# Attention with 16 heads: the scores of a pair's two heads issued in turns on the two halves of the array's rows

## The chip, the core and the metric

The kernel runs on one core of a Trainium2 chip. A core has TensorE (PE, matmuls and transpositions, results go to PSUM), VectorE (DVE), ScalarE (ACT), GpSimd (POOL) and a queue that starts DMAs (SP). The metric is the time of one execution on the device in microseconds (us): the median of three runs before the change is 2080.74 us (2080.17 to 2080.78).

## What is computed

Two transformer-like blocks run one after the other on 512 tokens of width 1024. The change is in one stage of the second block, an attention with 16 heads of 64 columns. Instead of a softmax it takes, for every query, products of sigmoids over the keys that lie between a key and the query ("stick breaking"):

```python
z = jnp.einsum("bhqd,bhkd->bhqk", qb, k32) * scale
mask = key_pos[None, :] < q_pos[:, None]
log_beta = jax.nn.log_sigmoid(z)
log_1m = jnp.where(mask, jax.nn.log_sigmoid(-z), 0.0)
suffix = lax.cumsum(log_1m, axis=3, reverse=True) - log_1m
wts = jnp.where(mask, jnp.exp(log_beta + suffix), 0.0)
return jnp.einsum("bhqk,bhkd->bhqd", wts, v32)
```

The output of all heads is then multiplied with `w_out` and added to the residual `x`. The mask is strictly causal, so a block of 128 queries needs only the key blocks up to its own.

## The kernel before

Activations lie transposed, features on the 128 partitions and the 512 tokens in the free dimension. All matmuls of weights are made three times over parts of numbers (`hi` and `lo` of type float32r): `mm3` issues lo times hi, hi times lo, hi times hi. A slab of 1024x128 weights is loaded by SP (`raw`), copied to `whi` by ACT (L101) and reduced to `wlo` by DVE (L102). `Feed` holds the order of all slabs and runs two to three ahead.

The attention stage works on pairs of heads: pair k (0 to 7) is one slab of 128 columns of q, of k and of v, and a head of it is one half of the 128 partitions (`p0 = 64 * half`). For each pair there are these steps:

- `proj(k, w)`: 24 matmuls of 128x512 (trace names `psmm`) for q and k; v is the same in two parts of 12 (`psv`). `evac` (L1164 to L1172) takes the result out of PSUM: ACT and DVE make `qh`, `ql`, `kh`, `kl`, and the tile `qk`.
- `scores(half, ...)`: for one head 12 matmuls with 64 rows into three PSUM tiles `z0`, `z1`, `z2` (L1119): three each over 512, 384, 128 and 256 columns, 3840 in all. Behind each of the three groups of columns ACT makes sigmoids `om` and `be` (L1124), POOL masks the diagonal blocks (L1128), DVE scans (`pr`, L1131) and multiplies (`be`, L1134). This chain of one head is called its mixing below.
- `turn(be)`: 10 transpositions of 128x128 (`t`, L1146), taken out as `w0h` to `w2l` by ACT and DVE.
- `values(k, half, ...)`: 12 matmuls of 128 rows with v (`po`, L1157); only the head's 64 rows of the result are taken out (`Oh`, `Ol`, L1161 and L1162).
- `vparts(t)`: four transpositions of v (`pv`, L1182), taken out as `vh` (ACT) and `vl` (DVE).
- `out_part(m, ks)`: 21 or fewer matmuls of the output projection (`pso`), put in where the last pairs have nothing to project.

PSUM: the pool `pmm3` has two buffers with the tag `mm`, used in turns by the `psmm`, `psv`, `po` and `pv` tiles: a new tile waits until the tile two before it has been taken out. `psz` holds `z0` to `z2`, `t0` and `t1`, and `pn` one tile `nr` for `t2`.

The order on PE is the order of the code (`manual_schedule` for PE). The order on the other engines is set at build time by a scheduler with an estimated time line, and then stands; each engine works through its own queue in order.

In the loop before (L1200 to L1226) the two heads are shifted against each other: while PE turns and multiplies one head, the mixing of the other one runs. PE does, for a pair: scores of head 1, turn head 0, project the next k, values of head 0, half of the next v, scores of the next pair's head 0, turn head 1, the other half of v, project the q after next, values of head 1, `vparts`.

Of the kernel before, what the change touches and what calls it, by code (L numbers as in the profile page):

```python
# [9 lines left out]
F32 = mybir.dt.float32  # L10
# [6 lines left out]
P = 128  # L17
T = 512
KD = 8
# [34 lines left out]
def block_kernel(ctx: ExitStack, tc: tile.TileContext, xT, pT, cols, cst, wA, wBr, wO, w13, w2, wPG, wPL,  # L54
                 aIn, aRI, aO, bQKV, bO, f13, f2, outT, dbg=None, upto=99):
    nc = tc.nc
    V, S, G, TE = nc.vector, nc.scalar, nc.gpsimd, nc.tensor
# [10 lines left out]
    pn = ctx.enter_context(tc.tile_pool(name="pn", bufs=1, space=PSUM))  # L68
# [71 lines left out]
    feed = Feed()  # L140
# [18 lines left out]
    feed.add([aO[m] for m in range(KD)])  # L159
    feed.mark((0, 0, 1))  # L160
    ffn_plan(f13[0], f2[0])
    feed.add([bQKV[8], bQKV[9], bQKV[0], bQKV[10]])
    for k in range(KD - 1):
        feed.add([bQKV[9 + 2 * (k + 1)], bQKV[k + 1]] + ([bQKV[8 + 2 * (k + 2)]] if k < KD - 2 else []))
    feed.mark((2, 0, 0, 1))
    feed.add([bO[m] for m in range(KD)])
    feed.mark((0, 0, 1))
# [9 lines left out]
    def gemm(pool, src, xs, tag="mm"):  # L177
        hi, lo = feed.next(src)
        ps = pool.tile([P, T], F32, tag=tag, name="psmm")
        mm3(ps, [(hi[:, k, :], lo[:, k, :], xs[k]) for k in range(len(xs))])  # L180
        return ps
# [106 lines left out]
    with ExitStack() as ca:  # L288
# [297 lines left out]
        for h in range(H):  # L586
            p0 = (h % 2) * 64
            Sm = ML.tile([P, 1280], F32, tag="Sm", bufs=1, name="Sm")
            for j in range(NB):
                w = T - j * P  # L590
# [481 lines left out]
    with ExitStack() as cs:  # L1072
# [27 lines left out]
        def parts(name, src, w, bufs):  # L1100
            hi = SB.tile([P, w], F32R, tag=name + "h", bufs=bufs, name=name + "h")
            lo = SB.tile([P, w], F32R, tag=name + "l", bufs=bufs, name=name + "l")
            S.copy(hi[:, 0:w], src)
            V.tensor_tensor(lo[:, 0:w], src, hi[:, 0:w].bitcast(F32), op=ALU.subtract)
            return hi, lo

        def scores(half, qp, kp):

            p0 = 64 * half
            zs = [psz.tile([P, T], F32, tag=f"z{g}", name=f"z{g}") for g in range(3)]  # L1110
            be = SB.tile([P, 1280], F32, tag="be", bufs=2, name="be")
            om = SB.tile([P, 1280], F32, tag="om", bufs=2, name="om")
            pr = SB.tile([P, 1280], F32, tag="pr", bufs=1, name="pr")
            for g in range(3):
                qbs = [(i, o, w) for g_, i, o, w in QB if g_ == g]
                for i, o, w in qbs:
                    qs = slice(p0, p0 + 64), slice(i * P, (i + 1) * P)
                    for n, (a, b) in enumerate(((0, 1), (1, 0), (0, 0))):
                        TE.matmul(zs[g][:, o:o + w], qp[a][qs], kp[b][p0:p0 + 64, 0:w], start=(n == 0 and o == 0),  # L1119
                                  stop=(n == 2), skip_group_check=True)  # L1120
                c0, cw = ZW[g]
                for t, n in ((om, 1), (be, 0)):
                    for i, o, w in qbs:
                        S.activation(t[:, c0 + o:c0 + o + w], zs[g][:, o:o + w], AF.Sigmoid, scale=rq[:, n, i:i + 1])  # L1124

                    d0 = c0 + qbs[0][1] + qbs[0][2] - P
                    d = t[:, d0:c0 + cw].rearrange("p (n c) -> p n c", c=P)
                    G.affine_select(d, d, pattern=[[0, len(qbs)], [-1, P]], base=0, channel_multiplier=1,  # L1128
                                    compare_op=ALU.is_gt, fill=float(n))
                sl = slice(c0, c0 + cw)  # L1130
                V.tensor_tensor_scan(pr[:, sl][:, ::-1], om[:, sl][:, ::-1], anew[:, sl][:, ::-1], 1.0,  # L1131
                                     op0=ALU.mult, op1=ALU.max)

                V.tensor_tensor(be[:, c0:c0 + cw - 1], be[:, c0:c0 + cw - 1], pr[:, c0 + 1:c0 + cw], op=ALU.mult)  # L1134
            return be

        def turn(be):

            out = []
            for g, (w, js) in enumerate(ZG):  # L1140
                t = pn.tile([P, T], F32, tag="nr", name="t2") if g == 2 else psz.tile([P, T], F32, tag=f"t{g}", name=f"t{g}")
                for j in js:
                    for i in range(j, NB):
                        c = next(ZW[g_][0] + o for g_, i_, o, _ in QB if i_ == i) + j * P
                        o = ZP[j][1] + (i - j) * P
                        TE.transpose(t[:, o:o + P], be[:, c:c + P], ident)  # L1146
                out.append(parts(f"w{g}", t[:, 0:w], w, 1))
            return out

        def values(k, half, wts, vp, pool=pmm, tag="mm"):  # L1150
            po = pool.tile([P, T], F32, tag=tag, name="po")
            n = 0
            for g in range(3):
                for j in ZG[g][1]:
                    o = ZP[j][1]
                    for (a, b) in ((1, 0), (0, 1), (0, 0)):
                        TE.matmul(po[:, j * P:], vp[a][:, j, :], wts[g][b][:, o:o + NW[j]], start=(n == 0), stop=(n == 11),  # L1157
                                  skip_group_check=True)
                        n += 1
            s_ = slice(64 * half, 64 * half + 64)  # L1160
            S.copy(O[k][0][s_], po[s_])  # L1161
            V.tensor_tensor(O[k][1][s_], po[s_], O[k][0][s_].bitcast(F32), op=ALU.subtract)  # L1162
# [4 lines left out]
        def evac(ps, w):  # L1167

            if w == 0:
                return parts("q", ps, T, 2)  # L1170
            t = tp.tile([P, T], F32, tag="xin", bufs=3, name="qk")
            V.tensor_tensor(t, ps, R, op=ALU.mult)  # L1172
            return t if w == 2 else parts("k", t, T, 2)

        def proj(k, w):

            return evac(gemm(pmm, bQKV[8 + 2 * k + w] if w < 2 else bQKV[k], A), w)

        def vparts(t):
            pv = pmm.tile([P, NB, P], F32, tag="mm", name="pv")  # L1180
            for b in range(NB):
                TE.transpose(pv[:, b, :], t[:, b * P:(b + 1) * P], ident)  # L1182
            return [x.rearrange("p (b d) -> p b d", b=NB) for x in parts("v", pv.rearrange("p b d -> p (b d)"), T, 2)]
# [3 lines left out]
        def out_part(m, ks, pool=pmm, tag="mm"):  # L1187

            if m not in part:
                part[m] = feed.next(bO[m]) + (pool.tile([P, T], F32, tag=tag, name="pso"),)  # L1190
            hi, lo, ps = part[m]
            mm3(ps, [(hi[:, c, :], lo[:, c, :], O[c]) for c in ks], first=ks[0] == 0, last=ks[-1] == KD - 1)

        with tc.manual_schedule(engines={mybir.EngineType.PE}):
            q, kk = proj(0, 0), proj(0, 1)
            vt = proj(0, 2)
            wa = scores(0, q, kk)
            qn = proj(1, 0)
            v = vparts(vt)
            for k in range(KD):  # L1200
                more = k < KD - 1
                wb = scores(1, q, kk)
                wt = turn(wa)
                if more:
                    kk, q = proj(k + 1, 1), qn
                    values(k, 0, wt, v)
                    vhi, vlo = feed.next(bQKV[k + 1])
                    pv = pmm.tile([P, T], F32, tag="mm", name="psv")
                    mm3(pv, [(vhi[:, c, :], vlo[:, c, :], A[c]) for c in range(4)], last=False)
                    wa = scores(0, q, kk)  # L1210
                    wt = turn(wb)
                    mm3(pv, [(vhi[:, c, :], vlo[:, c, :], A[c]) for c in range(4, 8)], first=False)
                    vt = evac(pv, 2)
                    if k < KD - 2:
                        qn = proj(k + 2, 0)
                    else:
                        out_part(0, range(0, 6))
                    values(k, 1, wt, v)
                    v = vparts(vt)
                else:  # L1220
                    out_part(1, range(0, 7))
                    values(k, 0, wt, v, psz, "z0")
                    out_part(0, range(6, 7))
                    wt = turn(wb)
                    out_part(2, range(0, 7), psz, "z1")
                    values(k, 1, wt, v, psz, "z0")  # L1226
            out_part(3, range(0, 7), psz, "z2")
            for m in range(4):
                out_part(m, range(7, 8))
        ss = SumSq("ss7")  # L1230
        for m in range(KD):
            ps = part[m][2] if m in part else gemm(psz, bO[m], O, tag=("z0", "t0", "t1", "z1")[m % 4])
            V.tensor_tensor(x_tiles[m], ps, x_tiles[m], op=ALU.add)
            split_scaled(A[m], x_tiles[m], col("nf1", m))
            ss.add(x_tiles[m])
# [168 lines left out]
```

## Time and profile before

| | before |
|---|---|
| median of three runs | 2080.74 us |
| the profiled execution, time | 2082.17 us |
| its span | 2080.2 us |
| PE busy | 2051.9 us (99%) |
| DVE busy | 1104.5 us (53%) |
| ACT busy | 763.9 us (37%) |
| POOL busy | 257.1 us (12%) |
| the chain of work that ended last | PE 91%, DVE 5%, ACT 1%, rest below |

The profile is of one execution. Busy time counts what an engine executes; matmuls are pipelined, so the pace of PE is read from the distance of starts, not from the duration of one. The granted clock says at which share of 2.4 GHz PE ran (0.5 is 1.2 GHz). The attention stage is the stretch from the first score matmul at 1451.17 us to the last partial output product, after which the rest of the output projection begins at 1683.42 us.

### The profile page before, as it was taken

The numbers are of one execution on the slowest core, as the hardware profiler recorded it, in microseconds if no ns is written. First come the engines' busy times: TensorE is split into PE (matmuls) and PEld (weight loads), VectorE is DVE, ScalarE is ACT, GpSimd is POOL, SyncE is SP. The second block draws the span as 40 slices with busy tenths as digits, with TensorE's granted clock in tenths as the row PEclk, the third lists the DMA queues.
The fourth block names the chain that finished last, engine by engine and source line by source line (L and its number), as shares of the span: only waits on it lengthen the run. The fifth ranks groups of instructions, "written<-read, shape, count | busy, mean of one in ns | idle before, by whom it ended". The sixth has DMA issues, their size and how long they took to land.

```text
span 2080.2 us, 24373 instructions
## 1 busy us (share of the span) xinstructions
PE 2051.9 (99%) x9786; PEld 1705.2 (82%) x9786; DVE 1104.5 (53%) x1455; ACT 763.9 (37%) x1099; POOL 257.1 (12%) x266
## 2 busy tenths in 40 slices
PE   8999999999999999999899999999999999999998
PEld 7778899888888888887788888888888888888887
DVE  5667453554444423669964444333877754444322
ACT  4334232333232322546642323223555533322221
POOL 0111000131000000252320000001322220000011
PEclk9999999999999999999999999999999999999999
DMA  4211111343333333322323333333122123333332
GB/s 168 71 55 59 60 41 43 105 127 101 97 96 100 91 97 98 114 79 82 91 91 96 97 101 92 92 101 98 55 61 72 41 77 96 91 102 94 92 102 68
DMA packets 53664, 181.69 MB, mean 87 GB/s; under 512 B 5808, under 2 KB 7984, under 8 KB 53552
## 3 DMA queue, kind: packets, MB, share of 16 engines
q1 hardware_dynamic: 53408, 180.05, 28.9%
q8 instruction: 76, 1.25, 0.3%
q14 instruction: 36, 0.29, 0.0%
q10 hardware_dynamic: 144, 0.10, 0.0%
HBM read 178.03 MB, written 2.10 MB: 87 GB/s over the span
## 4 chain that ended last, share of the span: by engine, by line
PE 91%; DVE 5%; ACT 1%; issue 1%; POOL 1%; DMA 1%; SPq 0%; POOLq 0%; DVEq 0%; ACTq 0%
PE psmm L173 19%; PE psmm L174 19%; PE psmm L175 19%; PE psd L173 6%; PE psd L175 6%; PE psd L174 6%; PE z L1119 2%; PE po L1157 1%; DVE wlo L102 1%; PE pU L731 1%; PE pX L726 1%; PE t L1146 1%; DVE xc L987 1%; PE psv L173 1%; PE psv L174 1%
## 5 line engine op out<-in xcount | busy, mean ns | idle before, releaser
L101 ACT CAST whi<-raw 128x1024 fp32r<-128x1024 f32 (+1 forms) x333 | 344.5, 1036 | 942.3 <-issue 374.5
L102 DVE TENSOR_TENSOR wlo<-raw,whi 128x1024 fp32r<-128x1024 f32 (+1 forms) x333 | 411.0, 1235 | 287.9 <-ACT whi L101 287.8
L173 PE MATMUL psmm<-Bh,wlo 128*128 128x512 f32 x1032 | 402.3, 390 | 0.3 <-DVE Ol L1162 0.3
L174 PE MATMUL psmm<-Bl,whi 128*128 128x512 f32 x1032 | 402.2, 390 | 0.1
L175 PE MATMUL psmm<-Bh,whi 128*128 128x512 f32 x1032 | 402.1, 390 | 0.0
L173 PE MATMUL psmm<-Ah,wlo 128*128 128x512 f32 x832 | 332.9, 401 | 2.8 <-DVE wlo L102 1.9
L175 PE MATMUL psmm<-Ah,whi 128*128 128x512 f32 x832 | 325.2, 391 | 0.0
L174 PE MATMUL psmm<-Al,whi 128*128 128x512 f32 x832 | 324.4, 390 | 0.6 <-DVE Al L189 0.6
L173 PEld LDWEIGHTS psmm<-Bh,wlo 128*128 128x128 f32 x1032 | 193.8, 188 | 40.8 <-DVE Ol L1162 0.5
L175 PEld LDWEIGHTS psmm<-Bh,whi 128*128 128x128 f32 x1032 | 193.8, 188 | 40.3
L174 PEld LDWEIGHTS psmm<-Bl,whi 128*128 128x128 f32 x1032 | 193.8, 188 | 40.2 <-DVE Bl L189 0.5
L216 POOL TENSOR_TENSOR ss<-ss,sq 128x512 f32<-128x512 f32 x55 | 85.6, 1561 | 1141.7 <-issue 803.7
L173 PE MATMUL psd<-Hh,wlo 128*128 128x512 f32 x506 | 196.8, 389 | 0.0
L174 PE MATMUL psd<-Hl,whi 128*128 128x512 f32 x506 | 196.8, 389 | 0.0
L175 PE MATMUL psd<-Hh,whi 128*128 128x512 f32 x506 | 196.8, 389 | 0.0
L173 PEld LDWEIGHTS psmm<-Ah,wlo 128*128 128x128 f32 x832 | 156.3, 188 | 36.0 <-DVE wlo L102 3.2
L175 PEld LDWEIGHTS psmm<-Ah,whi 128*128 128x128 f32 x832 | 156.1, 188 | 33.6
L174 PEld LDWEIGHTS psmm<-Al,whi 128*128 128x128 f32 x832 | 156.6, 188 | 30.3 <-DVE Al L189 1.1
L870 DVE TENSOR_TENSOR u<-psmm,R 128x512 f32<-128x512 f32 x66 | 45.6, 691 | 194.2 <-PE psmm L175 194.2
L866 DVE TENSOR_TENSOR s<-psmm,R 128x512 f32<-128x512 f32 x66 | 45.7, 692 | 137.0 <-PE psmm L175 134.0
L175 PEld LDWEIGHTS psd<-Hh,whi 128*128 128x128 f32 x506 | 95.0, 188 | 19.8
L174 PEld LDWEIGHTS psd<-Hl,whi 128*128 128x128 f32 x506 | 95.0, 188 | 19.8
(468 smaller groups left out, 2475.9 us busy)
## 6 DMA issues: line engine op xcount, KB each, us to landing
raw<-in_f SPq DMA_DIRECT2D x120, 512.0 KB, 3.6
raw<-in_w SPq DMA_DIRECT2D x60, 512.0 KB, 3.5
raw<-in_wA SPq DMA_DIRECT2D x43, 512.0 KB, 3.5
raw<-in_bQKV SPq DMA_DIRECT2D x24, 512.0 KB, 3.5
raw<-in_aIn SPq DMA_DIRECT2D x16, 512.0 KB, 3.6
raw<-in_f SPq DMA_DIRECT2D x16, 384.0 KB, 3.1
x<-in_xT SPq DMA_DIRECT2D x16, 256.0 KB, 3.6
raw<-in_wBr SPq DMA_DIRECT2D x8, 512.0 KB, 3.5
```

What stands on the lines that cost most here:

```text
L101: copied[0] = S.copy(hi[:, :nk, :], raw[:, :nk, :])
L102: V.tensor_tensor(lo[:, :nk, :], raw[:, :nk, :], hi[:, :nk, :].bitcast(F32), op=ALU.subtract)
L173: TE.matmul(ps, l, xh, start=(first and i == 0), stop=False)
L174: TE.matmul(ps, h, xl, start=False, stop=False)
L175: TE.matmul(ps, h, xh, start=False, stop=(last and i == n - 1))
L216: eng.tensor_tensor(self.acc, self.acc, sq, op=ALU.add)
L726: heads(lambda h: TE.matmul(pX[:, h], Nm[:, h, :], odd(U)[:, h], start=True, stop=True))
L731: heads(lambda h: TE.matmul(pU[:, h], Tt[:, h, :], X[:, h], start=True, stop=True))
L866: V.tensor_tensor(s1, p1, R, op=ALU.mult)
L870: V.tensor_tensor(u, p3, R, op=ALU.mult)
L987: V.scalar_tensor_tensor(ac, cx[:, j:j + T], col("aconv", 4 * k + j), ac, op0=ALU.mult, op1=ALU.add)
L1119: TE.matmul(zs[g][:, o:o + w], qp[a][qs], kp[b][p0:p0 + 64, 0:w], start=(n == 0 and o == 0), stop=(n == 2), skip_group_check=True)
```

## The change

Scores of both heads are one function now. It issues each of a head's 12 matmuls followed by the same one of the other head: head 0 reads rows 0 to 63 of the array, head 1 rows 64 to 127. Each head has PSUM tiles of its own (`z00` to `z02`, and `z10`, `z11` with the tile `nr` of the pool `pn` as the sixth), which the turned weights use again (`bank`). The loop does both heads of a pair together: scores of both, `vparts`, the next q, the next k, turn head 0, half of v, turn head 1, the other half, values of head 0, values of head 1. The slabs of the feed follow this order: q, k, v of a pair. Buffers: the parts of q and k have one instead of two, the turned weights two instead of one. The last pair has seven-eighths of two output products where the next q and k would stand.

```diff
-    feed.add([bQKV[8], bQKV[9], bQKV[0], bQKV[10]])
-    for k in range(KD - 1):
...
+    for k in range(KD):
+        feed.add([bQKV[8 + 2 * k], bQKV[9 + 2 * k], bQKV[k]])
...
-        def scores(half, qp, kp):
-
-            p0 = 64 * half
-            zs = [psz.tile([P, T], F32, tag=f"z{g}", name=f"z{g}") for g in range(3)]
+        def bank(half, g, name):
+            if half and g == 2:
+                return pn.tile([P, T], F32, tag="nr", name=name)
+            return psz.tile([P, T], F32, tag=f"z{half}{g}", name=name)
+
+        def scores(qp, kp):
+
+
+            zs = [[bank(half, g, f"z{g}") for g in range(3)] for half in range(2)]
+            for g, i, o, w in QB:
+                for n, (a, b) in enumerate(((0, 1), (1, 0), (0, 0))):
+                    for half in range(2):
+                        p0 = 64 * half
+                        TE.matmul(zs[half][g][:, o:o + w], qp[a][p0:p0 + 64, i * P:(i + 1) * P], kp[b][p0:p0 + 64, 0:w],
+                                  start=(n == 0 and o == 0), stop=(n == 2), skip_group_check=True)
+            return [mix(z) for z in zs]
+
+        def mix(zs):
...
-                for i, o, w in qbs:
-                    qs = slice(p0, p0 + 64), slice(i * P, (i + 1) * P)
-                    for n, (a, b) in enumerate(((0, 1), (1, 0), (0, 0))):
-                        TE.matmul(zs[g][:, o:o + w], qp[a][qs], kp[b][p0:p0 + 64, 0:w], start=(n == 0 and o == 0),
-                                  stop=(n == 2), skip_group_check=True)
...
-        def turn(be):
+        def turn(half, be):
...
-                t = pn.tile([P, T], F32, tag="nr", name="t2") if g == 2 else psz.tile([P, T], F32, tag=f"t{g}", name=f"t{g}")
+                t = bank(half, g, f"t{g}")
...
-                out.append(parts(f"w{g}", t[:, 0:w], w, 1))
+                out.append(parts(f"w{g}", t[:, 0:w], w, 2))
...
-                return parts("q", ps, T, 2)
+                return parts("q", ps, T, 1)
...
-            return t if w == 2 else parts("k", t, T, 2)
+            return t if w == 2 else parts("k", t, T, 1)
...
-            q, kk = proj(0, 0), proj(0, 1)
-            vt = proj(0, 2)
-            wa = scores(0, q, kk)
-            qn = proj(1, 0)
-            v = vparts(vt)
+            q, kk, vt = proj(0, 0), proj(0, 1), proj(0, 2)
             for k in range(KD):
-                more = k < KD - 1
-                wb = scores(1, q, kk)
-                wt = turn(wa)
-                if more:
-                    kk, q = proj(k + 1, 1), qn
-                    values(k, 0, wt, v)
+                wa, wb = scores(q, kk)
+                v = vparts(vt)
+                if k < KD - 1:
+                    q, kk = proj(k + 1, 0), proj(k + 1, 1)
+                    ta = turn(0, wa)
                     vhi, vlo = feed.next(bQKV[k + 1])
                     pv = pmm.tile([P, T], F32, tag="mm", name="psv")
                     mm3(pv, [(vhi[:, c, :], vlo[:, c, :], A[c]) for c in range(4)], last=False)
-                    wa = scores(0, q, kk)
-                    wt = turn(wb)
+                    tb = turn(1, wb)
                     mm3(pv, [(vhi[:, c, :], vlo[:, c, :], A[c]) for c in range(4, 8)], first=False)
                     vt = evac(pv, 2)
-                    if k < KD - 2:
-                        qn = proj(k + 2, 0)
-                    else:
-                        out_part(0, range(0, 6))
-                    values(k, 1, wt, v)
-                    v = vparts(vt)
+                    values(k, 0, ta, v)
+                    values(k, 1, tb, v)
                 else:
+                    out_part(0, range(0, 7))
                     out_part(1, range(0, 7))
-                    values(k, 0, wt, v, psz, "z0")
-                    out_part(0, range(6, 7))
-                    wt = turn(wb)
-                    out_part(2, range(0, 7), psz, "z1")
-                    values(k, 1, wt, v, psz, "z0")
-            out_part(3, range(0, 7), psz, "z2")
+                    ta = turn(0, wa)
+                    tb = turn(1, wb)
+                    out_part(2, range(0, 7), psz, "z00")
+                    values(k, 0, ta, v, psz, "z10")
+                    values(k, 1, tb, v, psz, "z01")
+            out_part(3, range(0, 7), psz, "z02")
```

The tags of the remaining output products are renamed in the same way. What this makes of the engines' queues is shown at two places.

DVE before, from the last step on one pair's values to the mixing of the next head (`vl` are the low parts of v, `pr` a scan, `be` its product, `w0l` to `w2l` the low parts of turned weights, `Ol` of the output):

```order
L1162 TENSOR_TENSOR Ol_10407<-po,Oh_10406 64x512
L1104 TENSOR_TENSOR vl<-pv,vh 128x512
L1131 SCALAR_TENSOR_TENSOR pr<-om,anew 128x512
L1134 TENSOR_TENSOR be<-be,pr 128x511
L1131 SCALAR_TENSOR_TENSOR pr<-om,anew 128x512
L1134 TENSOR_TENSOR be<-be,pr 128x511
L1131 SCALAR_TENSOR_TENSOR pr<-om,anew 128x256
L1104 TENSOR_TENSOR w0l<-t_11230,w0h 128x512
L1134 TENSOR_TENSOR be<-be,pr 128x255
```

DVE now, at the same place:

```order
L1170 TENSOR_TENSOR Ol_10407<-po,Oh_10406 64x512 x2
L1139 SCALAR_TENSOR_TENSOR pr<-om,anew 128x512
L1142 TENSOR_TENSOR be<-be,pr 128x511
L1139 SCALAR_TENSOR_TENSOR pr<-om,anew 128x512
L1142 TENSOR_TENSOR be<-be,pr 128x511
L1139 SCALAR_TENSOR_TENSOR pr<-om,anew 128x256
L1142 TENSOR_TENSOR be<-be,pr 128x255
L1139 SCALAR_TENSOR_TENSOR pr<-om,anew 128x512 x2
L1139 SCALAR_TENSOR_TENSOR pr<-om,anew 128x256
L1103 TENSOR_TENSOR vl<-pv,vh 128x512
L1142 TENSOR_TENSOR be<-be,pr 128x511 x2
L1142 TENSOR_TENSOR be<-be,pr 128x255
```

`vl` stood ahead of the first scan and now stands behind six scans and three products. `vl` is what gives the PSUM tile `pv` back, and the tile of the next k projection is the one that takes its buffer.

ACT before, at the sigmoids of one head (`vh` are the high parts of v):

```order
L1161 CAST Oh_10406<-po 64x512
L1103 CAST vh<-pv 128x512
L1124 ACTIVATE om<-z_11186,rq 128x512
L1124 ACTIVATE be<-z_11186,rq 128x512
L1124 ACTIVATE om<-z_11187,rq 128x384
L1124 ACTIVATE om<-z_11187,rq 128x128
L1124 ACTIVATE be<-z_11187,rq 128x384
L1124 ACTIVATE be<-z_11187,rq 128x128
L1124 ACTIVATE om<-z_11188,rq 128x256
```

ACT now, from the outputs' high parts to the third group of head 0:

```order
L1169 CAST Oh_10406<-po 64x512 x2
L1132 ACTIVATE om<-z_11098,rq 128x512
L1132 ACTIVATE be<-z_11098,rq 128x512
L1132 ACTIVATE om<-z_11101,rq 128x512
L1132 ACTIVATE be<-z_11101,rq 128x512
L1132 ACTIVATE om<-z_11099,rq 128x384
L1132 ACTIVATE om<-z_11099,rq 128x128
L1132 ACTIVATE be<-z_11099,rq 128x384
L1132 ACTIVATE be<-z_11099,rq 128x128
L1132 ACTIVATE om<-z_11102,rq 128x384
L1132 ACTIVATE om<-z_11102,rq 128x128
```

The sigmoids of the two heads alternate by group (`z_11098`, `z_11099` are head 0, `z_11101`, `z_11102` head 1), and `vh` now comes after all sixteen of them.

## Rows read from the trace of the kernel before

**Rows 1.** Busy by stretch, stage and one pair: PE, PEld, DVE, ACT, POOL; clock; DMA.

```profile
1451.17:1683.42 232.25, 229.81 (x1178) 193.19 (x1177) 170.21 (x224) 122.91 (x241) 62.35 (x96) 0.99 0.18 53
1541.66:1569.10 27.44, 27.44 (x146) 23.27 (x145) 21.42 (x29) 15.32 (x31) 7.83 (x12) 1.00 0.20 57
```

**Rows 2.** Timeline of PE, one pair: start, duration in us, instruction; first of each step.

```profile
1541.66 0.50 PE L1119 MATMUL z<-kl,qh 64*128 64x512 f32 x1
...
1543.79 1.31 PE L1146 MATMUL t<-CST,be 128*128 128x128 f32 x10
1544.86 0.48 PE L173 MATMUL psmm<-Bh,wlo 128*128 128x512 f32 x1
...
1550.44 0.39 PE L1157 MATMUL po<-w0h,vl 128*128 128x512 f32 x1
...
1552.36 0.40 PE L173 MATMUL psv<-Bh,wlo 128*128 128x512 f32 x1
...
1555.20 0.49 PE L1119 MATMUL z<-kl,qh 64*128 64x512 f32 x1
...
1557.32 1.31 PE L1146 MATMUL t<-CST,be 128*128 128x128 f32 x10
...
1561.20 0.39 PE L173 MATMUL psmm<-Bh,wlo 128*128 128x512 f32 x1
...
1566.65 0.39 PE L1157 MATMUL po<-w0h,vl 128*128 128x512 f32 x1
...
1568.56 0.60 PE L1182 MATMUL pv<-CST,qk 128*128 128x128 f32 x4
1569.10 0.50 PE L1119 MATMUL z<-kl,qh 64*128 64x512 f32 x1
```

**Rows 3.** Timeline of DVE, same pair: the mixing of one head.

```profile
1542.97 0.69 DVE L1104 TENSOR_TENSOR vl<-pv,vh 128x512 fp32r<-128x512 f32 x1
1543.82 1.22 DVE L1131 TENSOR_TENSOR_SCAN pr<-om,anew 128x512 f32<-128x512 f32 x1 [0.15 <-POOL om L1128]
...
1545.96 1.42 DVE L1131 TENSOR_TENSOR_SCAN pr<-om,anew 128x512 f32<-128x512 f32 x1
...
1548.19 0.68 DVE L1131 TENSOR_TENSOR_SCAN pr<-om,anew 128x256 f32<-128x256 f32 x1
1548.79 0.66 DVE L1104 TENSOR_TENSOR w0l<-t,w0h 128x512 fp32r<-128x512 f32 x1
1549.37 0.41 DVE L1134 TENSOR_TENSOR be<-be,pr 128x255 f32<-128x255 f32 x1
```

**Rows 4.** Timeline of ACT, same pair: the sigmoids of one head.

```profile
1542.73 0.69 ACT L1124 ACTIVATE om<-z,rq 128x512 f32<-128x512 f32 x1 [0.21 <-PE z L1119]
...
1543.89 0.84 ACT L1124 ACTIVATE om<-z,rq 128x384 f32<-128x384 f32 x2
...
1545.32 0.51 ACT L1124 ACTIVATE om<-z,rq 128x256 f32<-128x256 f32 x1
```

**Rows 5.** Timeline of POOL, same pair: masks of the first and third group.

```profile
1543.49 0.29 POOL L1128 TENSOR_SCALAR_AFFINE_SELECT om<-om 128x128 f32<-128x128 f32 x1 [9.68 <-PE z L1119]
...
1546.27 1.21 POOL L1128 TENSOR_SCALAR_AFFINE_SELECT om<-om 128x128 f32<-128x128 f32 x1
```

**Rows 6.** Waits of PE over the whole span: total us, times, longest.

```profile
PE pr L173 <- DVE wlo L102: 4.7, 1, 4.7
PE psmm L173 <- DVE wlo L102: 2.5, 3, 1.6
PE pv L1182 <- DVE Ol L1162: 1.4, 1, 1.4
```

**Rows 7.** Busy by stretch, the two stretches at half clock; columns as in rows 1.

```profile
991.30:998.10 6.80, 5.94 (x14) 4.68 (x15) 6.80 (x9) 3.26 (x5) 1.93 (x1) 0.50 0.52 154
1653.50:1660.35 6.85, 6.85 (x26) 6.13 (x25) 5.13 (x6) 5.15 (x12) 3.64 (x6) 0.50 0.00 0
```

More of the change, by code (lines that the diff above doesn't have):

```diff
@@ L161, in block_kernel @@
     ffn_plan(f13[0], f2[0])
-    feed.add([bQKV[8], bQKV[9], bQKV[0], bQKV[10]])
-    for k in range(KD - 1):
-        feed.add([bQKV[9 + 2 * (k + 1)], bQKV[k + 1]] + ([bQKV[8 + 2 * (k + 2)]] if k < KD - 2 else []))
+    for k in range(KD):
+        feed.add([bQKV[8 + 2 * k], bQKV[9 + 2 * k], bQKV[k]])
     feed.mark((2, 0, 0, 1))
@@ L1231, in block_kernel @@
         for m in range(KD):
-            ps = part[m][2] if m in part else gemm(psz, bO[m], O, tag=("z0", "t0", "t1", "z1")[m % 4])
+            ps = part[m][2] if m in part else gemm(psz, bO[m], O, tag=("z10", "z11", "z01", "z00")[m % 4])
             V.tensor_tensor(x_tiles[m], ps, x_tiles[m], op=ALU.add)
```

## The prediction

> **What bounds the kernel now.** I read the busy time by stretch first: in the attention stage PE is busy 229.81 of 232.25 us, DVE 170.21 and ACT 122.91 [rows 1]. One pair in the middle takes 27.44 us, PE has no idle time in it, and DVE is busy 21.42 us of them. The DMA engines are used to 0.20 there, so loads are not what PE waits for. In the timeline of PE the reader is to see that the steps of a pair follow each other without a gap, so their lengths can be taken from start to start [rows 2]. Whatever leaves PE's queue there shortens the kernel one for one, and whatever makes PE wait lengthens it one for one. DVE has only some 6 us a pair to spare, so the question is where its work lies against PE's.
>
> **What the change removes.** The 12 score matmuls of one head take 2.12 us (1555.20 to 1557.32) [rows 2]. They cover 3840 columns with 64 rows. A projection streams 24x512 columns with all 128 rows in 5.45 us (1561.20 to 1566.65). So a column costs 0.55 ns with half of the rows and 0.44 ns with all of them: using half of the rows saves nothing, and the other half stands idle. If the two halves work at the same time, a pair of heads costs 2.12 us instead of 4.24. Over 8 pairs that is 8 x 2.12 = 17.0 us off PE. If they don't, nothing is saved. No row of before shows two matmuls on different halves of the rows next to each other, so these are the two ends; I take the first for the sum and keep the second as a case.
>
> The Trainium skill ("TensorE: Matmul & The Clock Gate", Part 3: Packing small matmuls) says that matmuls on different row groups run concurrently, with starts about 4 ns apart. By it the pair costs 2.12 us plus 12 x 0.004, an estimate from that page, and the saving is the 17.0 us. No run here shows it yet.
>
> A pair without any wait would now be: scores 2.12, four transpositions of v 0.54 (1568.56 to 1569.10), next q 5.58 (1544.86 to 1550.44, the longer of the two projections since it follows transpositions), next k 5.45, turn 1.07 (1543.79 to 1544.86), half of v 2.84 (1552.36 to 1555.20), turn and other half 3.88 (1557.32 to 1561.20), values of both heads 1.92 + 1.91 (1550.44 to 1552.36, 1566.65 to 1568.56) [rows 2]. Sum: 8.24 up to the start of the next k, 17.07 from there on, 25.31 together, against 27.44.
>
> **What the change adds: a wait of PE for `vl`.** The next k takes the PSUM buffer of `pv`, and `vl` on DVE is the last reader of `pv`. Before, `vl` stood ahead of the scans, and the next tile in that buffer was the `po` of head 0, 9.3 us behind `pv` (0.54 ahead of 1541.66, to 1550.44) [rows 2]. Now DVE comes to `vl` only after three scans and three products of head 0 and three scans of head 1. Everything is counted from the first score matmul (1541.66 in the rows).
>
> DVE's way: the first scan starts 2.16 us after it (1543.82). Scans and products of one head run to 1549.37 + 0.41, less 0.58 for the `w0l` that lies between: 5.38 us. The scans of the other head are 1.22 + 1.42 + 0.68 = 3.32, `vl` is 0.69 [rows 3]. Together 2.16 + 5.38 + 3.32 + 0.69 = 11.55 us. That is the lower end.
>
> ACT's and POOL's way: the sigmoids alternate between the heads, so the third `om` of head 0 has eight steps ahead of it instead of four. Four take 2.59 (1542.73 to 1545.32), and the first starts 1.07 after the score matmul; so it starts at 1.07 + 5.18 = 6.25 and ends at 6.76 [rows 4]. The mask on POOL takes 0.29 or, where it starts beside a scan, until that scan has ended (1546.27 to 1547.48, the scan from 1545.96 to 1547.38) 1.21 [rows 3, 5]. So the third scan starts at 7.2 to 8.1, where DVE's way would have it at 2.16 + 4.37 = 6.53. That puts `vl` 0.65 to 1.55 later: 12.2 to 13.1. I take 12.65 and 0.05 for the signal.
>
> Without the wait the next k would start at 8.24. The wait is 12.7 - 8.24 = 4.45 us a pair (3.3 to 4.9). It comes eight times: seven at a next k, and in the last pair at the second output product, which takes the same buffer. Behind the waiting matmul all of PE's queue stands: the k projection, both turns, v, the values and the next scores; and since the next scores start the next mixing, nothing makes up for it later. The period becomes 12.7 + 17.07 = 29.8 us, 2.3 more than before. The saving of 2.12 buys nothing, since the wait ends at a time that DVE sets: every us that the scores become shorter is a us more of waiting.
>
> What is late elsewhere: `be` of head 1 is done some 1.8 us after `vl` (two products and a short one), long before its turn. The `ql`, `wlo`, `w` and `Ol` steps then have 17 us, with about 10 us of work. I price them at nothing; if that cover were gone, the wait would be at the next scores.
>
> **The other edits**, at nothing (DVE and the DMA engines hide them): the same slabs are loaded in another order; one buffer for q and k suffices since the scores that read them end before the next `evac`; two for the turned weights, since both heads hold them at once. The old waits of PE in this stage (232.25 - 229.81 = 2.44 us [rows 1]) and the half-clock stretch of its last pairs belong to the old order and go.
>
> **The clock.** PE runs at half clock in two stretches. Ahead of the one was an idle time of 4.7 us, ahead of the other one of 1.4 us [rows 6, 7]. Each lasted 6.8 us, in which PE was busy 5.94 and 6.85 us at half speed: 3.0 and 3.4 us lost. The second one is in this stage and goes with the old order (-3.4). Eight new waits of about 4.45 us are of the size of the first, so I expect most of them to be followed by a stretch at 1.2 GHz. Up to 4.4 of its 6.8 us can fall into the wait itself, so a drop costs 1.2 to 3.4 us; I take 2.6, nearer to the two rows. The next k behind the wait is on the path, so this adds: 8 x 2.6 = 20.8.
>
> **The sum.** -17.0 (scores) - 2.4 (old waits) - 3.4 (old half-clock stretch) + 8 x 4.45 = 35.6 (new waits) = +12.8, and with 20.8 for the clock +33.6. The profiled execution has 2082.2 us against a median of 2080.7, a difference of 1.5 that I leave out: 2080.7 + 33.6 = 2114. Bounds of this case: with waits of 3.3 and drops of 1.2, 2080.7 - 22.8 + 26.4 + 9.6 = 2094; with 4.9 and 3.4, 2080.7 - 22.8 + 39.2 + 27.2 = 2124.
>
> **Rivals.**
> 1. *The halves don't overlap* (the change doesn't do what it says). Then scores of a pair take 4.24 and the next k could start at 10.36. The first group of head 0 is complete three matmuls of 512 columns later, some 0.8 us, so `vl` ends at 12.4 to 13.9, say 13.5: the wait is 3.1 us (2.0 to 3.6). Sum: -5.8 + 24.8 + 20.8 = +39.8, 2120; up to 2131 with 3.6 and 3.4. For it: no row shows an overlap. Against: nothing in the rows either.
> 2. *The waits come, but the clock stays.* Then +12.8 with overlap and +19.0 without: 2094 to 2100. For it: three waits for `wlo`, the longest 1.6 us, left no such stretch [rows 6]. Against: the wait of 4.7 us did, and one of 1.4 us too.
> 3. *Faster: `vl` does not hold PE.* The place is the start of the next k. If the PSUM buffer is free by 8.24 us, the wait is none and the sum is -17.0 - 2.4 - 3.4 = -22.8: 2058. It decides at `vl` being done 8.2 us after the first score matmul instead of 12.7; at 11.1 us (a wait of 2.85) gain and wait would cancel without the clock. For it: DVE is busy only 21.42 of 27.44 us. Against: DVE's own steps ahead of `vl`, added without any idle time, are 9.4 us from a first scan that can't start before 2.16.
>
> **How the numbers follow.** Waits with half clock and overlapping scores 0.52 (2114), the same without overlap 0.20 (2120), waits without half clock 0.13 (2094 to 2100), no wait 0.11 (2058), a wait of about 2.85 without half clock 0.04 (2081, three quarters of it within 0.2%). A measurement of this kernel tells some 0.2%, 4 us, from no change. Faster by more than that: 0.12. Within it: 0.03. Slower: 0.85. The range takes in the first three cases down to somewhat shorter waits and up to the end of rival 1: 2088 to 2131.
>
> **What would show it.** In the profile after: a wait of PE `psmm` for DVE `vl`, seven times some 4.5 us, and one of `pso`; a period of about 30 us without and 32 with the half clock, from the first score matmul of one pair to that of the next; in the stage a granted clock well under 0.99. The starts of score matmuls of the two halves should lie in pairs next to each other, 24 of them in about 2.1 us; 4.2 would be rival 1. Prediction wrong: no wait at the k projection, or a wait that names another instruction than `vl`, or a stage shorter than 232 us.

## The result

| | before | after |
|---|---|---|
| median | 2080.56 us (4 runs) | 2113.37 us (4 runs) |
| ratio | | 1.0159 (95% interval 1.0142 to 1.0177) |
| span of the profiled execution | 2080.2 us | 2111.4 us |
| attention stage, first score matmul to the last partial output product | 232.25 us | 263.09 us |

The change makes the kernel 32.8 us slower by the medians. The spans of the two profiled executions differ by 31.2 us; 30.8 us of that lie in the attention stage, and from the stage's end to the end of the kernel both take the same 396.8 us.

The busy time by stretch, of the kernel after (us of the stretch; busy time of PE, PEld, DVE, ACT, POOL with their instructions; granted clock; share of the DMA engines; GB/s): the stage, one pair in the middle, the next k projection of that pair, and a stretch at half clock. The first two answer to [rows 1], the last one to [rows 7].

```profile
1451.52:1714.61 263.09, 225.23 (x1178) 187.04 (x1177) 168.94 (x224) 121.77 (x241) 51.48 (x96) 0.93 0.16 47
1548.86:1580.45 31.59, 27.04 (x146) 22.53 (x146) 21.19 (x28) 15.15 (x30) 6.42 (x12) 0.95 0.17 50
1561.63:1568.80 7.17, 7.17 (x24) 5.70 (x25) 3.21 (x5) 0.00 (x0) 0.00 (x0) 0.76 0.26 73
1562.10:1565.50 3.40, 3.40 (x10) 2.63 (x9) 2.74 (x5) 0.00 (x0) 0.00 (x0) 0.51 0.00 0
```

PE is busy 225.23 us of the stage, 4.6 us less than before, and idle 37.9 us instead of 2.4. Its clock is 0.93 of full speed over the stage instead of 0.99. A pair takes 31.59 us here (31.4 to 32.8 over the seven pairs) instead of 27.44. DVE and ACT do as much for a pair as before.

Who PE waited for, of the kernel after (total us, times, longest), against [rows 6]:

```profile
PE psmm L172 <- DVE vl L1103: 32.2, 7, 4.8
...
PE pso L172 <- DVE vl L1103: 5.1, 1, 5.1
```

Both rows are new: seven waits of a projection for `vl` and one of an output product. They account for 37.3 of the 37.9 us of idle time.

The timeline of PE in the same pair, answering to [rows 2] (start, duration, instruction; `x2` are two in a row of one kind, and here they are one of each head, since a head has each kind and width only once):

```profile
1548.86 0.50 PE L1119 MATMUL z<-kl,qh 64*128 64x512 f32 x2
1549.20 0.39 PE L1119 MATMUL z<-kh,ql 64*128 64x512 f32 x2
...
1550.97 0.66 PE L1190 MATMUL pv<-CST,qk 128*128 128x128 f32 x4
1551.39 0.48 PE L172 MATMUL psmm<-Bh,wlo 128*128 128x512 f32 x1
...
1561.63 0.50 PE L172 MATMUL psmm<-Bh,wlo 128*128 128x512 f32 x1 [4.55 <-DVE vl L1103]
...
1568.80 1.25 PE L1154 MATMUL t<-CST,be 128*128 128x128 f32 x10
```

The score matmuls of both halves start in twos, and all 24 take 2.11 us (1548.86 to 1550.97), as long as 12 took before. Then come v's transpositions and the next q, and at the next k PE waits 4.55 us. That projection takes 7.17 us (1561.63 to 1568.80) instead of 5.45, because 3.4 us of it run at half clock.

The timeline of DVE over the same time, answering to [rows 3]:

```profile
1551.00 1.23 DVE L1139 TENSOR_TENSOR_SCAN pr<-om,anew 128x512 f32<-128x512 f32 x1 [0.73 <-POOL om L1136]
1552.35 0.76 DVE L1142 TENSOR_TENSOR be<-be,pr 128x511 f32<-128x511 f32 x1
1553.66 1.23 DVE L1139 TENSOR_TENSOR_SCAN pr<-om,anew 128x512 f32<-128x512 f32 x1 [0.55 <-POOL om L1136]
1555.12 0.87 DVE L1142 TENSOR_TENSOR be<-be,pr 128x511 f32<-128x511 f32 x1 [0.23 <-POOL be L1136]
1556.53 0.76 DVE L1139 TENSOR_TENSOR_SCAN pr<-om,anew 128x256 f32<-128x256 f32 x1 [0.54 <-POOL om L1136]
1557.39 0.51 DVE L1142 TENSOR_TENSOR be<-be,pr 128x255 f32<-128x255 f32 x1
1557.93 2.92 DVE L1139 TENSOR_TENSOR_SCAN pr<-om,anew 128x512 f32<-128x512 f32 x3
1560.88 0.69 DVE L1103 TENSOR_TENSOR vl<-pv,vh 128x512 fp32r<-128x512 f32 x1
```

Three scans and three products of head 0, three scans of head 1, then `vl`, which ends at 1561.57, 12.71 us after the first score matmul. PE starts the k projection 0.06 us later. Behind its first scan, head 0's mixing also waits three times for masks of POOL, 1.3 us together; ACT and POOL take the two heads' sigmoids and masks in turns.

### The profile page after: what moved, and what is told of

It reads as the page before. It is cut to its first block, busy times and chain, and to the rows that moved or that the text cites. A ratio compares the mean times of both kernels' runs of the same rounds, so it can differ in the third digit from the quotient of the medians.

```text
span 2111.4 us, 24340 instructions
## 1 busy us (share of the span) xinstructions
PE 2046.4 (97%) x9786; PEld 1698.2 (80%) x9786; DVE 1103.3 (52%) x1455; ACT 762.9 (36%) x1099; POOL 246.0 (12%) x266
## 4 chain that ended last, share of the span: by engine, by line
PE 89%; DVE 6%; POOL 2%; ACT 1%; issue 1%; DMA 1%; SPq 0%; POOLq 0%; DVEq 0%; ACTq 0%
PE psmm L172 19%; PE psmm L173 19%; PE psmm L174 19%; PE psd L172 5%; PE psd L173 5%; PE psd L174 5%; DVE pr L1139 2%; PE po L1165 1%; PE pU L730 1%; PE pX L725 1%; POOL be L1136 1%; DVE wlo L102 1%; PE t L1154 1%; DVE xc L986 1%; POOL om L1136 1%
## 5 line engine op out<-in xcount | busy, mean ns | idle before, releaser
L172 PE MATMUL psmm<-Bh,wlo 128*128 128x512 f32 x1032 | 409.2, 397 | 32.2 <-DVE vl L1103 32.2
L173 PE MATMUL psmm<-Bl,whi 128*128 128x512 f32 x1032 | 407.6, 395 | 0.1
L174 PE MATMUL psmm<-Bh,whi 128*128 128x512 f32 x1032 | 407.2, 395 | 0.0
L174 PEld LDWEIGHTS psmm<-Ah,whi 128*128 128x128 f32 x832 | 156.1, 188 | 33.6
```

The source lines that it names most:

```text
L172: TE.matmul(ps, l, xh, start=(first and i == 0), stop=False)
L173: TE.matmul(ps, h, xl, start=False, stop=False)
L174: TE.matmul(ps, h, xh, start=False, stop=(last and i == n - 1))
```

## The experiments

Theory 1 is that of the prediction: the overlapping scores do save PE time, and the change lost only by the wait for `vl` and the half clock behind it. Theory 2: two mixings at once are too much for DVE, ACT and POOL, and `vl` was only the place where it showed. Theory 3: issuing the halves in turns saves nothing. The first four kernels ran on one chip and the last two on another; the kernel before took 2080.41 us on the one and 2080.21 us on the other.

**v first.** The four transpositions of v are put ahead of the scores:

```diff
-                wa, wb = scores(q, kk)
                 v = vparts(vt)
+                wa, wb = scores(q, kk)
```

> The changed kernel with one line moved: the four transpositions of v stand ahead of the score matmuls of the pair instead of behind them, so that vl is queued on DVE ahead of the first scan. Theory 1 (the wait for vl and the half clock behind it are all that the change lost; the overlapping scores did save 17 us): no wait for vl, no stretch at half clock in the attention stage, a pair takes 25.3 us, 2080.6 - 22.8 = 2058 us (2054 to 2063). Theory 2 (two mixings at once are more than DVE, ACT and POOL can do between the scores and the turns, and vl was only the place where it showed): the wait moves to the turns or to the next scores, 2081 us or more.

Measured: 2061.2 us, ratio to before 0.9905 (0.9888 to 0.9921). In the stretches (the stage, one pair) and the waits of PE within the stage:

```profile
1453.50:1662.69 209.19, 208.12 (x1173) 176.17 (x1173) 165.72 (x223) 122.72 (x240) 51.41 (x96) 1.00 0.20 59
1529.22:1554.46 25.24, 25.24 (x146) 21.51 (x145) 20.90 (x28) 15.40 (x31) 6.43 (x12) 1.00 0.22 65
```

```profile
PE psmm L172 <- DVE wlo L102: 0.6, 1, 0.6
PE po L1165 <- DVE qk L1180: 0.5, 1, 0.5
```

No wait for `vl` is left, the clock is at 1.00 throughout, and a pair takes 25.24 us without idle time on PE. The stage is 23.1 us shorter than before and 53.9 us shorter than with the change as it was. Theory 2 falls: the same two mixings at once, with DVE busy 20.90 of 25.24 us, cost PE no more than the two short waits above in the whole stage. In the timeline of DVE, up to the last scan of head 1 it is only `vl` that has another place:

```profile
1530.23 0.69 DVE L1103 TENSOR_TENSOR vl<-pv,vh 128x512 fp32r<-128x512 f32 x1
1531.36 1.22 DVE L1139 TENSOR_TENSOR_SCAN pr<-om,anew 128x512 f32<-128x512 f32 x1 [0.44 <-POOL om L1136]
```

The median is 3 us above the expected one, though the stage is as short as expected (232.25 - 22.8 = 209.45): the first scores begin at 1453.50 instead of 1451.17. Of these 2.3 us, 1.4 are a wait for the first pair's v and its transpositions, which stand ahead of the first scores now. This version is faster than both kernels.

**v first, heads one after the other.** As before this, with all 12 score matmuls of head 0 issued before those of head 1:

```diff
-            for g, i, o, w in QB:
-                for n, (a, b) in enumerate(((0, 1), (1, 0), (0, 0))):
-                    for half in range(2):
+            for half in range(2):
+                for g, i, o, w in QB:
+                    for n, (a, b) in enumerate(((0, 1), (1, 0), (0, 0))):
```

> As the run with v first, but the 12 score matmuls of head 0 are issued first and then the 12 of head 1, so that no two neighbours use different halves of the rows, except one. Theory 1: the scores of a pair take 4.2 us instead of 2.1, nothing waits, 8 x 2.1 = 17 us more than with v first: 2075 us (2071 to 2080). Theory 3 (the halves turn by turn save nothing by themselves; what became shorter is something else in the order): the same time as with v first.

Measured: 2073.13 us, 0.9962 (0.9947 to 0.9977). The stage:

```profile
1453.91:1674.63 220.72, 219.68 (x1174) 187.44 (x1173) 170.60 (x223) 121.89 (x240) 60.42 (x96) 1.00 0.19 56
```

It is 11.5 us longer than with turns, and a pair's scores take 3.63 us (from the first score matmul at 1534.11 to the next projection at 1537.74) instead of 2.12. So theory 3 falls: the turns are worth 1.51 us a pair, 12 us in all. The expected 4.2 us were too many. The timeline of PE shows why, at the passage from head 0 to head 1 in the middle:

```profile
1534.11 0.49 PE L1119 MATMUL z<-kl,qh 64*128 64x512 f32 x1
...
1535.62 0.27 PE L1119 MATMUL z<-kh,qh 64*128 64x128 f32 x1
1535.63 0.50 PE L1119 MATMUL z<-kl,qh 64*128 64x512 f32 x2
1535.90 0.45 PE L1119 MATMUL z<-kh,ql 64*128 64x256 f32 x2
...
1537.74 0.50 PE L172 MATMUL psmm<-Bh,wlo 128*128 128x512 f32 x1
```

From 1535.63 on, matmuls of 512 columns belong to head 1 and those of 256 to the end of head 0 (a row of two shows the width of its first). Head 1's first matmul starts 0.01 us behind head 0's ninth, although three more of head 0 are issued ahead of it. Head 1's 12 then take their full 2.11 us (1535.63 to 1537.74), but they begin 0.6 us before the 2.12 us of head 0 are over (1534.11 + 2.12 = 1536.23).

**v behind, heads one after the other.** The changed kernel with the same edit of the three loops.

> The changed kernel with the scores of head 0 issued before those of head 1, v behind them as in the changed kernel. Theory 1: the scores take 2.1 us more a pair, the wait for vl becomes shorter by most of that (3.1 instead of 4.6 us), since DVE sets when it ends; a pair takes 0 to 1 us more, 2113 to 2122 us in all. Theory 3 or a chain in which the length of the scores counts fully: 17 us more, 2130 us.

Measured: 2114.21 us, 1.0161 (1.0146 to 1.0176); against the changed kernel's 2113.37 no difference. The waits of PE:

```profile
PE psmm L172 <- DVE vl L1103: 24.9, 7, 3.8
...
PE pso L172 <- DVE vl L1103: 4.1, 1, 4.1
```

The stage:

```profile
1452.34:1715.50 263.16, 233.50 (x1177) 195.51 (x1177) 171.86 (x224) 121.94 (x241) 60.68 (x96) 0.94 0.16 47
```

The scores of a pair take 3.62 us, 8 x 1.5 = 12 us more in all, and the stage is as long as with the change (263.16 against 263.09 us). The waits fall from 37.3 to 29.0 us, less than the scores grow, since `vl` comes some 0.5 us later within a pair. The rest is the clock: PE is busy only 8.3 us longer (233.50 against 225.23), since six waits instead of eight brought a stretch at half clock in this execution. So what the turns save came back, 8.3 us as waiting, as theory 1 has it, and some 4 us at half clock: the same edit is worth 12 us where nothing waits for `vl` and nothing measurable where PE does.

**The wait filled with work.** The changed kernel with 18 matmuls ahead of each next q projection, whose result the projection overwrites:

```diff
+        def proj_twice(k, n):
+
+            hi, lo = feed.next(bQKV[8 + 2 * k])
+            ps = pmm.tile([P, T], F32, tag="mm", name="psmm")
+            for _ in range(n):
+                TE.matmul(ps, hi[:, 0, :], A[0][0], start=True, stop=True)
+            mm3(ps, [(hi[:, c, :], lo[:, c, :], A[c]) for c in range(KD)])
+            return evac(ps, 0)
...
-                    q, kk = proj(k + 1, 0), proj(k + 1, 1)
+                    q, kk = proj_twice(k + 1, 18), proj(k + 1, 1)
```

> The changed kernel with 18 more matmuls of 128x512 ahead of each next q projection (seven times), into the same PSUM tile, which the projection then begins anew: 18 x 0.227 = 4.1 us of PE work that changes no result and lies in the time in which PE waits for vl. Theory 1 with the clock as a cost of the idle time: the seven stretches at half clock go, the wait shrinks from 4.6 to some 0.5 us, the period of a pair falls from 32.1 to 29.9 us, 2113.4 - 7 x 2.2 = 2098 us (2095 to 2101), faster with more work. Rival (the half clock comes from the score matmuls on half of the rows, not from the idle time): the stretches stay, 2113 us or more.

Measured: 2100.48 us, 1.0094 (1.0079 to 1.011): 12.9 us less than the changed kernel, with 126 matmuls more. The stretches (the stage, one pair) and the waits of PE:

```profile
1451.64:1701.24 249.60, 240.30 (x1303) 200.99 (x1303) 168.94 (x224) 122.03 (x241) 51.49 (x96) 0.99 0.16 49
1541.95:1571.95 30.00, 29.54 (x163) 24.79 (x162) 21.19 (x28) 15.18 (x30) 6.41 (x12) 1.00 0.17 53
```

```profile
PE pso L172 <- DVE vl L1103: 5.1, 1, 5.1
...
PE psmm L172 <- DVE vl L1103: 3.6, 7, 0.7
```

A pair takes 30.0 us at full clock instead of 31.4 to 32.8. The score matmuls on half of the rows are the same, so it was the idle time that cost the clock. The one stretch at half clock that is left in the stage comes with the one long wait that is left, that of the last pair.

**By block of columns.** v first, with three matmuls of head 0 and then three of head 1 for each of the four blocks of columns:

```diff
-                for n, (a, b) in enumerate(((0, 1), (1, 0), (0, 0))):
-                    for half in range(2):
+                for half in range(2):
+                    for n, (a, b) in enumerate(((0, 1), (1, 0), (0, 0))):
```

> As the run with v first, but each block of columns is issued as three matmuls of head 0 and then three of head 1, so that only at 7 places of a pair two neighbours use different halves. Theory 1 with overlap of direct neighbours alone: of the 7680 columns of a pair 4 x one matmul of 512, 384, 128, 256 and 3 x one of 384, 128, 128 run beside another, 1920 columns of 0.44 ns = 0.85 us; the scores take 3.63 - 0.85 = 2.8 us, 8 x 0.65 more than with v first: 2066 us (2064 to 2069). If the array takes a later matmul of the other half ahead of its turn, 2061 us as with v first; if only long runs in strict turns overlap, 2073 us as in the serial one.

Measured: 2061.35 us, the same as v first with strict turns (2061.2). In the timeline of PE the matmuls stand in twos, although three of a head are issued in a row:

```profile
1555.87 0.50 PE L1119 MATMUL z<-kl,qh 64*128 64x512 f32 x2
1556.21 0.40 PE L1119 MATMUL z<-kh,ql 64*128 64x512 f32 x2
1556.44 0.40 PE L1119 MATMUL z<-kh,qh 64*128 64x512 f32 x2
1556.67 0.35 PE L1119 MATMUL z<-kl,qh 64*128 64x384 f32 x2
...
1558.00 0.50 PE L172 MATMUL psmm<-Bh,wlo 128*128 128x512 f32 x1
```

The first assumption, that only direct neighbours overlap, was wrong. Matmuls of the other half start ahead of their turn: head 1's first of a block ahead of two of head 0 that are issued before it, and ahead of three in the serial run above. There, with twelve of a head in a row, only the end of one head overlapped with the start of the other.

**v later.** The changed kernel with the transpositions of v behind the next q and k:

```diff
                 wa, wb = scores(q, kk)
-                v = vparts(vt)
                 if k < KD - 1:
                     q, kk = proj(k + 1, 0), proj(k + 1, 1)
+                    v = vparts(vt)
...
                 else:
+                    v = vparts(vt)
```

> The changed kernel with the transpositions of v moved the other way, behind the next q and k projections. vl comes even later on DVE, behind both mixings, but then the k projection takes the buffer of the last values and q that of the first, and the half of the next v is the next to need the buffer of pv. Theory 1 (what costs is which tile takes the buffer whose last reader is queued behind the mixing, not a late vl): no wait at the k projection, one of about 1 us at the first half of v, no half clock: 2061 + 8 x 1 = 2069 us (2061 to 2077). If a late vl costs by itself, or DVE can't keep up with two mixings at once, 2100 us or more.

Measured: 2076.85 us, 0.9981 (0.9972 to 0.999), at the upper end of what was expected. The waits of PE within the stage:

```profile
PE psv L172 <- DVE qk L1180: 6.4, 7, 0.9
PE pso L172 <- DVE vl L1103: 5.1, 1, 5.1
```

DVE in the pair whose first score matmul starts at 1531.94:

```profile
1547.25 0.69 DVE L1180 TENSOR_TENSOR qk<-psmm,R 128x512 f32<-128x512 f32 x1
...
1548.98 0.69 DVE L1103 TENSOR_TENSOR vl<-pv,vh 128x512 fp32r<-128x512 f32 x1
```

`vl` is queued behind both mixings here and ends 17.7 us after the first score matmul, 5 us later than in the changed kernel, and yet the k projection does not wait. What waits is the next half of v, 0.9 us each time, and not for `vl` but for the `qk` of k, which is queued ahead of it. So the expectation had the size of this wait right and its buffer wrong: counted two tiles back, the half of v takes the buffer of k, and that of `pv` goes to the values of head 0, which come later. A pair takes 26.7 us, some 1.4 more than with v first; 0.9 of it is this wait, and the rest is spread over the steps. The last pair keeps its old order and with it the wait of 5.1 us, which brought a stretch at half clock of 3.4 us that the expectation did not have. So a late `vl` does not hold PE by itself; it cost because the tile that took its buffer stood on PE's path.

## Why the prediction was right

The forecast was 2114 us, the median is 2113.37. By its steps:

- *A pair's scores take 2.12 us with both halves at work.* Measured 2.11, and 12 us of difference against the serial order. The Trainium skill ("TensorE: Matmul & The Clock Gate", Part 3: Packing small matmuls) had said that matmuls on different row groups run concurrently; the trace agrees, with 24 of them in 2.11 us. By the prediction's estimate from that page, 2.12 + 12 x 0.004, it is 16.6 us that would come off and not 17.0; the 2.11 measured shows no such addition. Rival 1 is out. But 4.24 us, which the prediction set against 2.12, is not what the two heads cost one after the other: that took 3.63, since head 1 begins 0.6 us before head 0 is done. So of the 17.0 us that the sum takes off, 12 come from the turns and 5 come already from putting the two heads next to each other.
- *`vl` ends 12.65 us after the first score matmul.* Measured 12.71. Two errors cancel in it: head 0's mixing took 6.90 us (1551.00 to 1557.90) where the sum had 5.38 + 1.1, and the three scans of head 1 took 2.95 instead of 3.32, with nothing between them. The third scan was forecast at 7.2 to 8.1 and came at 7.67 (1556.53).
- *Eight waits of 4.45 us, 35.6 together.* Measured eight, 32.2 + 5.1 = 37.3 us.
- *Waits bring half clock, 8 x 2.6 = 20.8 us.* Each of the eight brought one, as forecast, but five of the eight stretches lasted 3.4 us and three 6.8. The seven k projections took 6.98 to 8.34 us instead of 5.45, 15.3 us more together, and the output product 6.3 instead of 5.0: 16.6 us, 2.1 each. The size came from two rows of 6.8 us [rows 7], and this term was 4 us too large.
- *The old waits (2.4) and the old stretch at half clock (3.4) go.* Both are gone.

With these sizes the sum is -17.0 - 2.4 - 3.4 + 37.3 + 16.6 = +31.1 us, against +30.8 in the stage. The mechanism was right in each term. That the median was met within 1 us is in part luck: the forecast of +33.6 is 2.8 above what the stage shows, mostly since the clock was put 4.2 too high and the waits 1.7 too low, and the two medians lie 32.8 us apart where the profiled spans lie 31.2 apart. Rival 2 (no half clock) is out by the clock of 0.93, rival 3 (nothing waits) by the row of `vl`. But its price, 2058 us, is nearly what the kernel costs when the wait is taken away: 2061.2. So the saving was real, and the place of one line cost 53.9 us of the stage: the 37.3 of waiting and the 16.6 at half clock. The other edits were put at nothing, and none shows in a wait.

The size of 6.8 us for a stretch at half clock was a matter of luck too. Two waits of equal length, of the kernel after (the stretch with its clock, the first matmul behind the wait):

```profile
1528.00:1534.82 6.82, 5.95 (x14) 4.69 (x15) 4.05 (x7) 0.00 (x0) 0.00 (x0) 0.50 0.25 71
1592.85:1596.26 3.41, 3.04 (x7) 2.46 (x8) 3.41 (x6) 0.00 (x0) 0.00 (x0) 0.50 0.00 0
```

```profile
1528.87 0.79 PE L172 MATMUL psmm<-Bh,wlo 128*128 128x512 f32 x1 [4.55 <-DVE vl L1103]
1593.22 0.80 PE L172 MATMUL psmm<-Bh,wlo 128*128 128x512 f32 x1 [4.55 <-DVE vl L1103]
```

Both waits last 4.55 us. In the first the clock falls 0.87 us before PE goes on and the stretch lasts 6.8 us; in the second it falls 0.37 us before and lasts 3.4. All 16 stretches that came with a wait for `vl` in these runs go the same way: the seven in which the clock fell 0.9 to 2.1 us before PE went on lasted 6.8 us, the nine in which it fell between 0.5 us before and 0.5 us after lasted 3.4. Nor does the code set the length: the wait of 4.7 us near 992 us, which stands in all eight kernels, brought 3.4 us in four of the traces and 6.8 us in the other four. The old stretch of this stage does not fit: there the clock fell 0.95 us after PE had gone on behind a wait of 1.4 us, and the stretch lasted 6.8 us. The two rows of 6.8 us [rows 7] were two samples from one execution.

What stays open: what decides when the clock falls, and why two of the eight waits of 3.5 to 4.1 us in the serial order brought no stretch at half clock.

## What to carry to other kernels

When an order is changed, read for each PSUM buffer which tile takes it next and where the last reader of the old tile stands in its engine's queue; a small step that a scheduler queues behind a long chain holds whatever takes its buffer. A step made shorter on the bottleneck gives nothing if the next wait ends at a time that another engine sets: first look for what ends last behind the step. Two halves of the rows in turns took 1.5 us off the 3.6 us of a pair's products over 64 rows here. A wait of some us on PE can cost half clock on top, here 2 us for each wait of 4.5 to 5.1 us; a price for that needs stretches from more than one execution.

## What the runs showed of the hardware beyond what was expected

- Matmuls on the other half of the rows start ahead of their place in the order of issue, which is that of the code: with three of head 0 issued ahead of three of head 1 the 24 took 2.13 us (1555.87 to 1558.00), as with strict turns. In the serial order the first of head 1 started with the ninth of head 0. So PE does not work strictly in that order there.
- 18 matmuls more for each of seven pairs made the kernel 12.9 us faster, because PE then kept its full clock (1.00 over a pair instead of 0.95).
- A stretch at half clock was 3.4 us long in five of eight cases and 6.8 us in three, behind waits of nearly the same length; the long ones were those in which the clock fell earlier in the wait.
